# A hybrid layer on one core: the first stage's loads, transposes, modulations and products in another order

## The chip, the cores and the metric

The kernel runs on one core of a Trainium2 chip. The core has a matrix engine (TensorE; PE in the rows, with its weight loads as PEld), a vector engine (VectorE, DVE), a scalar engine (ScalarE, ACT), a general engine (GpSimd, POOL) and SyncE (SP), which here only issues transfers. Each engine works through its own list of instructions in order; semaphores join them. All loads and stores of this stage go through SyncE's queue to the core's 16 DMA engines. The metric is the device time of one execution in microseconds (us), the median of several runs.

## The reference

One layer of a two-branch backbone. 256 context tokens and 1024 latent tokens of width 1024 are RMS-normed and modulated, and one projection gives the columns of an mLSTM head group and of a windowed attention head group. Behind it come both mixers, the output projection, a gated feed-forward mixer and a final norm. The part that the change touches:

```python
sh_a, sc_a, g_a, sh_f, sc_f, g_f = jnp.split((silu(c) @ w_ada + b_ada), 6)      # latent
csh_a, csc_a, ... = jnp.split(silu(c_ctx) @ w_ada + b_ada, 6)                   # context
hc = modulate(rmsnorm(ctx, norm_mix), csh_a, csc_a)     # h * (1 + scale) + shift
hx = modulate(rmsnorm(x, norm_mix), sh_a, sc_a)
u  = h @ w_in      # columns: q/k, v, o, gates of the mLSTM, q, k, v of the attention
```

All in float32. The matrix products are done as three products of halves: every operand is split into a high part (rounded to the engine's faster 32-bit format) and the low rest, and hi*hi + hi*lo + lo*hi are summed (`mm3`).

## The kernel before, in words

The 1280 tokens are ten tiles of 128: tiles 0 and 1 are context, 2 to 9 latent. The first stage, lines 206 to 409, goes as follows. `x_load` brings a tile (0.5 MB) into one of six buffers. `x_norm` squares and sums it on ScalarE, takes the root, and scales the tile on VectorE. `x_trans` turns its eight 128x128 blocks on TensorE into two PSUM banks of the pool `pl` (four banks), and `x_evac` copies the two banks to the transposed store `xT`, one on ScalarE, one on VectorE. `ada_load` brings the modulation weights in pieces (n, q) of 1 MB: n = 0 and 1 are the two halves of the shift, n = 2 and 3 those of the scale, q a half of the contraction. `ada_mm` multiplies a piece with the two conditioning vectors into half of a PSUM pair of the pool `pk`; `ada_vec` turns the row of results into a column per feature (`modS`, `modG`).

`modulate(half, grp, ks)` then makes the projection's operand for one half of the features and one group of tokens (group 0: tiles 0 and 1; group 1: tiles 2 to 5; group 2: tiles 6 to 9): the high part on ScalarE, the full value on VectorE for blocks 1 and 3 of the four and on GpSimd for 0 and 2, and the low part as VectorE's subtraction. Both halves of `modulate` need shift and scale of their features, so half 0 needs n = 0 and 2. `px_mm(c, kts)` multiplies tile c with the small projection weights `w_x` (272 columns: gates, attention keys and values), three matmuls per block of features, 24 per tile; K0 is half 0 and K1 half 1. `px_out(c)` adds the gate bias, copies keys and values out of PSUM into one of three buffers `kv`, rotates the keys on GpSimd, and stores the buffer to memory (`kv_d`). `load_split` loads a weight in two pieces and cuts each into high part (ScalarE) and low part (VectorE).

Among the instructions of the two `manual_schedule` blocks the order is the written one, for each engine of the block: TensorE, VectorE, ScalarE and GpSimd to the end of the stage, SyncE in the inner block only (in the kernel before, to line 385). What is written behind the blocks is placed by the framework's planner, which works with a model of the durations and may put such instructions between those of a block: eight products of the next stage run between those of tiles 7 and 8. The banks: tiles 0, 1 and 6 to 9 use the two banks of the pool `pd`, tiles 2 to 5 those of `pl`. The next stage, `dense`, line 522, starts with a product in `pd` (line 540, tile `pc_`) and then the keys' product in the pair of `pk` (line 548, tile `pp`); its weights come through `load_split` too, in line with the stores on SyncE's queue.

## Time and profile before

| | |
|---|---|
| Time, median of 3 runs | 1319.99 us (1316.4 to 1323.47) |
| The profiled execution | 1321.8 us, span 1319.8 us |
| TensorE busy | 1260.1 us, 95% of the span |
| VectorE, ScalarE, GpSimd busy | 74%, 48%, 20% |
| Mean granted clock of TensorE | 0.985 of full |
| Chain that ended last | TensorE 71%, VectorE 10%, DMA 4%, ScalarE 4%, issue 3% |

The busy share of an engine is an average over stages with different limits; the stage of the change is the first 90 us. The chain is followed back from the last instruction, at each step to what released it. The granted clock is the share of TensorE's clock that it was given: 1.0 is 2.4 GHz, 0.5 is 1.2 GHz.

### The profile page before, as it was taken

The numbers are of one execution on the slowest core, as the hardware profiler recorded it, in microseconds if no ns is written. First come the engines' busy times: TensorE is split into PE (matmuls) and PEld (weight loads), VectorE is DVE, ScalarE is ACT, GpSimd is POOL, SyncE is SP. The second block draws the span as 40 slices with busy tenths as digits, with TensorE's granted clock in tenths as the row PEclk, the third lists the DMA queues.
The fourth block names the chain that finished last, engine by engine and source line by source line (L and its number), as shares of the span: only waits on it lengthen the run. The fifth ranks groups of instructions, "written<-read, shape, count | busy, mean of one in ns | idle before, by whom it ended". The sixth has DMA issues, their size and how long they took to land.

```text
span 1319.8 us, 19433 instructions
## 1 busy us (share of the span) xinstructions
PE 1260.1 (95%) x7047; PEld 1070.9 (81%) x7047; DVE 981.3 (74%) x1752; ACT 636.1 (48%) x1295; POOL 258.8 (20%) x252
## 2 busy tenths in 40 slices
PE   5889999999898999999989999999999999999997
PEld 4689998989898777778768788888888888788886
DVE  4644677767675788997798877777777776877887
ACT  6532546454674566676664333333333333434435
POOL 0450000000035133332420222222122223001000
PEclk8899999999899999999999999999999999999999
DMA  9431435353135412121432323232222326984553
GB/s 362 160 116 33 126 96 176 105 168 101 49 114 164 171 51 96 65 81 48 150 118 67 123 104 112 106 107 99 90 102 106 118 96 218 344 290 158 202 200 134
DMA packets 90225, 175.63 MB, mean 133 GB/s; under 512 B 12746, under 2 KB 29330, under 8 KB 90130
## 3 DMA queue, kind: packets, MB, share of 16 engines
q1 hardware_dynamic: 89842, 173.61, 39.0%
q8 instruction: 55, 0.90, 0.3%
q10 hardware_dynamic: 288, 0.79, 0.2%
q14 instruction: 40, 0.33, 0.1%
HBM read 136.04 MB, written 38.33 MB: 132 GB/s over the span
## 4 chain that ended last, share of the span: by engine, by line
PE 71%; DVE 10%; DMA 4%; ACT 4%; issue 3%; POOL 2%; SPq 0%; ACTq 0%; POOLq 0%; DVEq 0%
PE pd L1857 14%; PE pa L1349 8%; PE pc L1349 8%; PE pp L548 5%; PE pe L1349 4%; PE pd L1349 4%; PE pb L1349 4%; PE u L1119 2%; PE pv L299 2%; PE pv L301 2%; PE pv L300 2%; PE po L299 2%; PE po L301 2%; PE po L300 1%; DVE nm L1067 1%
## 5 line engine op out<-in xcount | busy, mean ns | idle before, releaser
L1451 ACT CAST wh<-Rb 128x1024 fp32r<-128x1024 f32 (+1 forms) x66 | 59.5, 904 | 144.7 <-PE pd L1349 81.6
L1857 PE MATMUL pd<-dh,al 128*128 128x512 f32 x296 | 115.4, 390 | 1.1 <-DVE al L1223 1.1
L1857 PE MATMUL pd<-dl,ah 128*128 128x512 f32 x296 | 115.3, 389 | 0.0
L1857 PE MATMUL pd<-dh,ah 128*128 128x512 f32 x296 | 115.2, 389 | 0.0
L1349 PE MATMUL pc<-hB,wh 128*128 128x512 f32 x344 | 106.0, 389 | 1.1 <-DVE av L1428 1.1
L1349 PE MATMUL pa<-hB,wh 128*128 128x512 f32 x336 | 103.5, 389 | 0.0
L1239 DVE TENSOR_TENSOR wl<-Rb,wh 128x1024 fp32r<-128x1024 f32 (+1 forms) x66 | 68.9, 1045 | 39.4 <-ACT wh L1451 38.8
L1559 POOL TENSOR_TENSOR tt<-vt,tt 128x512 f32<-128x512 f32 x22 | 29.5, 1341 | 321.8 <-ACT tt L1553 321.8
L548 PE MATMUL pp<-hl,wh 128*128 128x512 f32 x256 | 79.3, 405 | 0.0
L1349 PEld LDWEIGHTS pc<-hB,wh 128*128 128x128 f32 x344 | 64.6, 188 | 15.0 <-DVE av L1428 1.6
L299 PE MATMUL pv<-wh,hl 128*128 128x256 f32 x256 | 75.9, 296 | 0.0
L1349 PEld LDWEIGHTS pa<-hB,wh 128*128 128x128 f32 x336 | 63.0, 188 | 13.5 <-ACT sn L1523 0.4
L301 PE MATMUL pv<-wh,hl 128*128 128x256 f32 x256 | 72.4, 283 | 0.0
L300 PE MATMUL pv<-wl,hl 128*128 128x256 f32 x256 | 72.3, 282 | 0.0
L820 POOL TENSOR_TENSOR ta<-z,rope 128x256 f32<-128x256 f32 x16 | 14.3, 895 | 288.7 <-ACT z L816 288.7
L1349 PE MATMUL pc<-hB,wl 128*128 128x512 f32 x172 | 66.9, 389 | 0.0
L1857 PEld LDWEIGHTS pd<-dh,al 128*128 128x128 f32 x296 | 55.6, 188 | 13.4 <-DVE al L1223 1.8
L1349 PE MATMUL pa<-hB,wl 128*128 128x512 f32 x168 | 65.4, 389 | 0.0
L1857 PEld LDWEIGHTS pd<-dl,ah 128*128 128x128 f32 x296 | 55.6, 188 | 11.9 <-DVE dl L1223 0.3
L1857 PEld LDWEIGHTS pd<-dh,ah 128*128 128x128 f32 x296 | 55.6, 188 | 11.4
L299 PE MATMUL px<-wh,hl 128*128 128x256 f32 (+1 forms) x192 | 59.6, 311 | 2.9 <-ACT kr L322 2.9
L301 PE MATMUL px<-wh,hl 128*128 128x256 f32 (+1 forms) x192 | 56.7, 295 | 1.4 <-DVE hl L295 1.4
(1067 smaller groups left out, 3829.2 us busy)
## 6 DMA issues: line engine op xcount, KB each, us to landing
w<-in_w_ada_dram SPq DMA_DIRECT2D x64, 256.0 KB, 2.7
br<-in_w_down_dram SPq DMA_DIRECT2D x25, 512.0 KB, 6.0
Ra<-in_w_up_dram SPq DMA_DIRECT2D x22, 512.0 KB, 3.6
Rb<-in_w_up_dram SPq DMA_DIRECT2D x22, 512.0 KB, 3.6
ar<-act_s SPq DMA_DIRECT2D x44, 256.0 KB, 3.3
act_a<-tt SPq DMA_DIRECT2D x33, 256.0 KB, 2.0
act_s<-tt SPq DMA_DIRECT2D x33, 256.0 KB, 2.0
wr<-in_w_h_dram SPq DMA_DIRECT2D x16, 512.0 KB, 4.5
```

What stands on the lines that cost most here:

```text
L299: T.matmul(ps, st_hi, mv_hi, start=first, stop=False)
L300: T.matmul(ps, st_hi, mv_lo, start=False, stop=False)
L301: T.matmul(ps, st_lo, mv_hi, start=False, stop=last)
L548: T.matmul(pp[:, 512 * n:512 * n + 512], wkq[sw][:, kt, cs], hl[n][part][:, kt, :], start=kt == 0 and sw + part == 0, stop=kt == KT - 1 an ...
L820: G.tensor_tensor(out=ta[:].rearrange("p (h e) -> p h e", h=4), in0=q4, in1=rp_(1), op=ALU.mult)
L1067: V.tensor_reduce(out=self.nm[:, j:j + 1], in_=self.sv[j], axis=AX.X, op=ALU.max, negate=True)
L1119: T.matmul(self.u[:], vv[:, c, self.g], part[i][:, kk * 2 * P:(kk + 1) * 2 * P], start=kb + m == 0, stop=kb == last and m == 1)
L1239: sub = lambda e, o, x, y: e.tensor_tensor(out=o, in0=x, in1=y, op=ALU.subtract)
L1349: T.matmul(ps[:], wt[sw][:, j, ks], hB[part][:, blk, kt, :], start=first and kt == 0 and sw + part == 0, stop=last and kt == 3 and sw == 1 ...
L1451: S.copy(wt[0][:], src)
L1559: G.tensor_tensor(out=self.tt[:, h2_], in0=self.vt[:], in1=self.tt[:, h2_], op=ALU.mult)
L1857: T.matmul(ps[:], ac[sa][:, js], w[sw], start=first and n == 0, stop=last and n == 2, skip_group_check=not fresh)
```

## The change

The loads stand in another order: tiles 0 to 5, then both pieces of n = 0, half the weights `w_x`, both pieces of n = 2, the other half, then tiles 6 to 9, n = 1 and n = 3. Norm, transposes and copies of tiles 6 to 9 stand behind the first products of tiles 0 to 3. The weights' two halves are cut at two places. `spin(n)` issues n transposes of the identity matrix into a bank of `pl` that nothing reads; 12, 5 and 7 of them stand ahead of and between the products and rows of n = 2. The order of the four blocks in a product is 1, 3, 0, 2. Tiles 6 and 7 accumulate in the pair of `pk` that held the rows of n = 1 and 3, tiles 8 and 9 in `pl`. The inner block, with SyncE's written order, now reaches to the last product of tile 7 and so takes in the stores of tiles 0 to 5; behind it the products of tiles 8 and 9 are written with the outputs between them.

```diff
@@ -138,7 +138,7 @@
 
     st = p1.enter_context(tc.tile_pool(name="st", bufs=2))
 
-    def load_split(src, w, rawf=None, split=True, alloc=True):
+    def load_split(src, w, rawf=None, split=True, alloc=True, now=range(2)):
         room = lambda: [st.tile([P, KT, XW], F32R, name=n, tag=n)[:].rearrange("p a b -> p (a b)")[:, :KT * w]
                         .rearrange("p (k f) -> p k f", k=KT) for n in ("wh", "wl")]
         hi, lo = room() if alloc else (None, None)
@@ -158,7 +158,7 @@
                 load(q)
                 cut(q)
             return hi, lo
-        for q in range(2):
+        for q in now:
             load(q)
 
         def rest(qs=range(2)):
@@ -168,6 +168,7 @@
             for q in qs:
                 cut(q)
             return hi, lo
+        rest.load = load
         return rest
 
 
@@ -217,16 +218,17 @@
         V.reciprocal(rstd[:, c:c + 1], rstd[:, c:c + 1])
         V.tensor_scalar(out=xi[:], in0=xi[:], scalar1=rstd[:, c:c + 1], scalar2=None, op0=ALU.mult)
 
-    def x_trans(c):
-        xi = xis.pop(c)
-        for q in range(2):
+    def x_trans(c, qs=range(2)):
+        xi = xis[c]
+        for q in qs:
             pts[c, q] = pl.tile([P, 4, P], F32, name="pt", tag="l")
             for k in range(4):
                 kt = 4 * q + k
                 T.transpose(pts[c, q][:, k, :], xi[:, kt * P:(kt + 1) * P], ident[:])
 
-    def x_evac(c):
-        for q, e in enumerate((S.copy, V.tensor_copy)):
+    def x_evac(c, qs=range(2)):
+        for q in qs:
+            e = (S.copy, V.tensor_copy)[q]
             e(xT[:, 4 * q:4 * q + 4, c * P:(c + 1) * P], pts.pop((c, q))[:])
 
     def bc(ap, n):
@@ -303,12 +305,16 @@
     pxs = {}
 
     def px_mm(c, kts):
-        if kts[0] == 0:
-            pool, tag = (pl, "l") if 2 <= c < 6 else (pd, "d")
-            pxs[c] = pool.tile([P, 512], F32, name="px", tag=tag)
+        if c not in pxs:
+            if c in (6, 7):
+
+                pxs[c] = pas[-1][:, 512 * (c - 6):512 * (c - 6) + 512]
+            else:
+                pool, tag = (pl, "l") if c >= 2 else (pd, "d")
+                pxs[c] = pool.tile([P, 512], F32, name="px", tag=tag)
         px = pxs[c]
         for kt in kts:
-            mm3(px[:, :XW], hsl(0, kt, c), hsl(1, kt, c), wX[0][:, kt, :], wX[1][:, kt, :], kt == 0, kt == KT - 1)
+            mm3(px[:, :XW], hsl(0, kt, c), hsl(1, kt, c), wX[0][:, kt, :], wX[1][:, kt, :], kt == K0[0], kt == K1[-1])
 
     def px_out(c):
         px = pxs.pop(c)
@@ -331,82 +337,111 @@
             G.tensor_tensor(out=kvv[:, :, 1], in0=tv[:, 1, :, 0], in1=tv[:, 0, :, 1], op=ALU.add)
         nc.sync.dma_start(kv_d[c], kv[:])
 
-    K0, K1 = range(4), range(4, 8)
+    K0, K1 = (1, 3, 0, 2), (5, 7, 4, 6)
+
+
+    def spin(n):
+        if "spin" not in pxs:
+            pxs["spin"] = pl.tile([P, 512], F32, name="spin", tag="l")
+        for _ in range(n):
+            T.transpose(pxs["spin"][:, 0:P], ident[:], ident[:])
+
     with tc.manual_schedule(engines={mybir.EngineType.PE, mybir.EngineType.DVE, mybir.EngineType.Activation,
                                      mybir.EngineType.Pool}):
         with tc.manual_schedule(engines={mybir.EngineType.SP}):
-            for c in range(3):
+            for c in range(6):
                 x_load(c)
-            ada_load(0, 0)
-            for c in range(3, 6):
-                x_load(c)
-            ada_load(0, 1)
+            ada_load(0, 0); ada_load(0, 1)
+            wX = load_split(I["w_x"], XW, split=False, alloc=False, now=(0,))
+            ada_load(2, 0); ada_load(2, 1)
+            wX.load(1)
             x_norm(0)
             x_norm(1); x_trans(0); x_evac(0)
             x_load(6)
             x_norm(2); x_trans(1); x_evac(1)
-            ada_mm(0, 0)
             x_load(7)
             x_norm(3); x_trans(2); x_evac(2)
-            x_load(8); ada_load(2, 0)
+            x_load(8)
             x_norm(4); x_trans(3); x_evac(3)
-            x_load(9); ada_load(2, 1)
-            wX = load_split(I["w_x"], XW, split=False, alloc=False)
+            x_load(9)
+            ada_mm(0, 0)
             x_norm(5); x_trans(4); x_evac(4)
             ada_mm(0, 1)
-            x_norm(6); x_trans(5); x_evac(5); ada_vec(0)
-            ada_load(1, 0); ada_load(1, 1); ada_load(3, 0); ada_load(3, 1)
+            x_trans(5); x_evac(5)
+            ada_load(1, 0); ada_load(1, 1)
+            wXf, wX = wX, wX((0,))
+            ada_vec(0)
+            spin(12)
+            ada_mm(2, 0)
+            ada_mm(2, 1)
+            spin(5)
+            ada_load(3, 0); ada_load(3, 1)
             nc.sync.dma_start(rw[:], I["rw"][0:1, 0:536].broadcast_to([P, 536]))
-            x_norm(7); x_trans(6); x_evac(6)
-            x_norm(8); x_trans(7); x_evac(7)
-            ada_mm(2, 0)
-            x_norm(9); x_trans(8); x_evac(8)
-            ada_mm(2, 1)
-            x_trans(9); x_evac(9); ada_vec(2)
+            nc.sync.dma_start(rope[:], I["rope"])
+            ada_vec(2)
+            spin(7)
             modulate(0, 0)
-            wX = wX()
+            px_mm(0, K0)
+            px_mm(1, K0)
+            modulate(0, 1)
+            x_norm(6)
+            px_mm(2, K0)
+            px_mm(3, K0)
+            x_norm(7)
+            x_trans(6); x_evac(6)
             ada_mm(1, 0)
-            px_mm(0, K0)
-            modulate(0, 1)
+            x_norm(8)
+            x_trans(7); x_evac(7)
+            x_norm(9)
             ada_mm(1, 1)
-            px_mm(1, K0)
+            x_trans(8); x_evac(8)
             ada_vec(1)
-            px_mm(2, K0)
             ada_mm(3, 0)
-            hl.append(hl_(1))
-            modulate(0, 2, (0, 1))
-            px_mm(3, K0)
-            ada_mm(3, 1)
-            px_mm(4, K0)
-            ada_vec(3)
-            px_mm(5, K0)
-            nc.sync.dma_start(rope[:], I["rope"])
+            x_trans(9); x_evac(9)
+            wXf((1,))
             wkq = load_split(I["w_h"][0, 0], 256, split=False)
             nc.sync.dma_start(tri[:], I["cst"][:, 1:3])
-        modulate(1, 0)
-        px_mm(0, K1)
-        px_mm(1, K1)
-        modulate(1, 1)
-        px_out(0)
-        px_mm(2, K1)
-        modulate(0, 2, (2, 3))
-        modulate(1, 2, (0, 1))
-        px_out(1)
-        px_mm(3, K1); px_out(2)
-        modulate(1, 2, (2, 3))
-        px_mm(4, K1); px_out(3)
-        wkq = wkq()
-        px_mm(5, K1); px_out(4)
-        px_out(5)
-        amf = xin.tile([P, D], F32, name="amf", tag="xi")[:, :2 * P].rearrange("p (a b) -> p a b", a=2)
-        nc.sync.dma_start(amf, I["cst"][:, 5:7])
+            hl.append(hl_(1))
+            px_mm(4, K0)
+            modulate(0, 2, (1, 3))
+            ada_mm(3, 1)
+            px_mm(5, K0)
+            ada_vec(3)
+            modulate(0, 2, (0, 2))
+            modulate(1, 0)
+            px_mm(6, K0)
+            px_mm(7, K0)
+            px_mm(0, K1)
+            px_mm(1, K1)
+            modulate(1, 1)
+            px_out(0)
+            px_mm(2, K1)
+            px_out(1)
+            px_mm(3, K1)
+            modulate(1, 2, (1, 3))
+            px_out(2)
+            px_mm(4, K1)
+            modulate(1, 2, (0, 2))
+            px_out(3)
+            px_mm(5, K1)
+            wkq = wkq()
+            px_out(4)
+            px_mm(6, K1)
+            px_out(5)
+            px_mm(7, K1)
+            amf = xin.tile([P, D], F32, name="amf", tag="xi")[:, :2 * P].rearrange("p (a b) -> p a b", a=2)
+            nc.sync.dma_start(amf, I["cst"][:, 5:7])
+        px_out(6)
+        px_mm(8, K0 + K1)
+        px_out(7)
         V.tensor_scalar(out=rwc("gain"), in0=rwc("gain"), scalar1=0.5, scalar2=None, op0=ALU.mult)
         V.tensor_copy(identr[:], ident[:])
+        px_mm(9, K0 + K1)
+        px_out(8)
         V.tensor_copy(identb[:], ident[:])
         V.tensor_copy(amask[:], amf)
         V.tensor_scalar(out=nsink[:], in0=rwc("sink"), scalar1=-1.0, scalar2=None, op0=ALU.mult)
-        for c in range(6, NCH):
-            px_mm(c, range(8)); px_out(c)
+        px_out(9)
     p0.close()
 
 
```

## Rows read from the trace of the kernel before

**Rows 1.** Windows. Columns: stretch, length, busy time of each engine (count), clock, DMA share, GB/s.
```profile
core 0: us, PE busy (x) PEld busy (x) DVE busy (x) ACT busy (x) POOL busy (x), PEclk, DMA share, GB/s
9.30:24.85 15.55, 12.16 (x80) 8.88 (x80) 9.83 (x21) 12.63 (x29) 0.00 (x0) 0.99 1.03 400
24.85:31.65 6.80, 6.21 (x28) 3.54 (x32) 4.04 (x8) 3.85 (x8) 0.00 (x0) 0.52 1.04 397
31.65:38.50 6.85, 3.89 (x33) 2.15 (x25) 4.71 (x11) 5.05 (x8) 3.75 (x4) 0.98 1.04 385
38.50:45.30 6.80, 6.25 (x27) 4.34 (x28) 5.43 (x8) 4.41 (x8) 3.31 (x2) 0.52 1.06 379
45.30:74.40 29.10, 27.01 (x207) 24.16 (x206) 17.05 (x34) 13.76 (x24) 12.40 (x15) 1.00 0.09 30
74.40:82.60 8.20, 5.28 (x34) 4.38 (x32) 2.04 (x11) 1.68 (x9) 5.09 (x13) 1.00 0.70 204
82.60:87.20 4.60, 4.59 (x24) 4.59 (x25) 1.53 (x2) 0.30 (x2) 3.50 (x8) 0.63 0.34 121
87.20:170.00 82.80, 82.80 (x568) 76.48 (x567) 46.21 (x134) 32.65 (x81) 3.11 (x4) 1.00 0.31 89
```

**Rows 2.** Timeline of the head: start, length, engine, line, operation; in brackets idle time before.
```profile
21.30 0.95 PE L270 MATMUL pa<-sel,ym 128*128 128x2 f32 x8
...
31.07 1.19 PE L261 MATMUL pa<-wa,ym 128*32 128x512 f32 x8
...
34.59 2.08 ACT L293 ACTIVATE hc<-xT,modS,modG 128x256 fp32r<-128x256 f32 x4 [1.11 <-DVE modG L276]
...
35.24 1.57 DVE L295 TENSOR_TENSOR hc<-ym,hc 128x256 fp32r<-128x256 f32 x3
...
37.71 0.39 PE L299 MATMUL px<-wh,hc 128*128 128x272 f32 x1 [2.23 <-ACT wh L153]
39.05 0.59 PE L300 MATMUL px<-wl,hc 128*128 128x272 f32 x1 [0.94 <-DVE wl L154]
```

**Rows 3.** Timeline of TensorE: steps of the operations; the last row from the chain.
```profile
20.37 1.09 PE L226 MATMUL pt<-ident,xi 128*128 128x128 f32 x8
...
40.12 0.43 PE L301 MATMUL px<-wh,hc 128*128 128x272 f32 x1
...
41.48 0.43 PE L301 MATMUL px<-wh,hc 128*128 128x272 f32 x1
...
48.40 1.06 PE L261 MATMUL pa<-wt,ym 128*32 128x512 f32 x8
...
62.07 0.29 PE L300 MATMUL px<-wl,hl 128*128 128x272 f32 x1
...
69.63 0.29 PE L300 MATMUL px<-wl,hl 128*128 128x272 f32 x1
...
90.27 9.09 PE pp L548 x40
```

**Rows 4.** Chain that ended last, the store behind tile 6's product: start, length, what.
```profile
77.20 4.83 DMA kv_d<-kv
```

**Rows 5.** Timeline of ScalarE and VectorE: squares of two tiles, scaling of one.
```profile
20.99 1.06 ACT L215 ACTIVATE ym<-xi 128x1024 bf16<-128x1024 f32 x1
...
22.84 1.06 ACT L215 ACTIVATE ym<-xi 128x1024 bf16<-128x1024 f32 x1
...
22.69 0.75 DVE L218 TENSOR_SCALAR xi<-xi,rstd 128x1024 f32<-128x1024 f32 x1
```

**Rows 6.** Issue of ada 2's first piece; its size and time from issue to landing.
```profile
16.09 0.43 SPq L250 DMA_DIRECT2D wa<-in_w_ada_dram  x1
...
wa<-in_w_ada_dram SPq DMA_DIRECT2D x1, 1024.0 KB, 8.0
```

**Rows 7.** Windows of transposes alone (line 226) and modulation products alone (line 261).
```profile
28.25:31.65 3.40, 1.97 (x8) 1.57 (x8) 0.54 1.02 394
...
28.25:31.65 3.40, 1.57 (x12) 0.20 (x8) 0.54 1.02 394
```

**Rows 8.** Waits of SyncE's queue: in total, times, longest.
```profile
SPq L149 <- DVE wl L154: 27.2, 3, 20.6
```

## The prediction

> **What bounds the kernel now.** I read the page first: TensorE is busy for 95% of a span of 1319.8 us, and it holds 71% of the chain that ended last. Any gain must therefore be time in which TensorE stands still or runs slowly. The edits lie in the first 90 us, so the second view is the table of windows over that stretch [rows 1]. From 87.20 on TensorE is busy without a gap (82.80 of 82.80 us at full clock): whatever moves 87.20 moves everything behind it by as much. Before 87.20 it is otherwise. The first product of the input projection starts at 37.71 [rows 2]; until then TensorE has done only transposes and the small modulation products.
>
> From 37.71 to the last projection product's end at some 87.2 are 49.5 us. Their work at full clock: 61 matmul starts lie between 62.07 and 69.63 [rows 3], so a projection matmul is 0.126 us, and 240 of them (10 token tiles x 24) are 30.3; three modulation halves (a row of eight matmuls is 1.06, some 1.0 start to start [rows 3]) 3.0; two of the small row products at some 0.8 each (0.95 with its tail [rows 2]) 1.6; and eight key products of the next stage, done early in a gap, 1.8 at 0.227 each (40 in 9.09 [rows 3]). Sum 36.7, so 12.8 us are lost. Where: from 38.50 to 45.30 the granted clock is 0.52, its lower level, 1.2 GHz [rows 1]; there a matmul takes 0.227 (six steps from 40.12 to 41.48 [rows 3]), which costs some 2.8 from 39.05 on. From 82.60 it is at 0.63 for 4.60 us, another 1.5. Idle time is 2.1 from 45.30 to 74.40 and 2.9 from 74.40 to 82.60 [rows 1], and 0.9 is the wait for the weights' low part, to 39.05 [rows 2]. The remaining 2.6 or so are short hand-overs between groups. The 2.9 are a chain, read in order of time: the two PSUM banks that the last four tiles share are freed by copies which wait for a buffer that a store has to empty, and that store took 4.83 us, to 82.03 [rows 4].
>
> Because the eight early key products are not lost work, the old start of the next stage counts as 87.2 - 1.8 = 85.4.
>
> **The head, in the new order.** The first six tiles run as before through the end of tile 5's transposes at 21.30 and the small row product behind it, to 22.25 [rows 2, 3]; only the place of a modulation product between tiles changes, and TensorE idles there anyway (12.16 busy of 15.55 [rows 1]). ScalarE has less to do: a token tile takes it 1.85 us (20.99 to 22.84 [rows 5]), and tiles 6 to 9 (7.4 us) move behind the first products. The cast and subtraction of half the projection weights, 1.1 + 1.5, take their place; both are over by some 25, before their user.
>
> Then comes the scale row (ada 2). Its data now has ahead of it six tiles of 0.524 MB, two pieces of 1.05, half the weights (0.557) and its own two pieces, with 0.16 of constants 8.06 MB. In the kernel before, the first piece of ada 2 had 8.03 MB up to its end and landed at 16.09 + 8.0 = 24.1 [rows 6]. So the second piece lands at some 24.2. Twelve idle transposes stand ahead: 8 transposes start to start are 0.93 (20.37 to 21.30 [rows 2, 3]), so 12 are 1.4, to 23.7; the first half ends at 24.7, and the second can start, its data just there. The transposes thus cost nothing at full clock; at half they take 2.8 and all starts some 2 us later. Later data would hide that too, so the bounds are 0 and +2; I take 0.
>
> From the start of the same second product to the modulation's start were 31.07 to 34.59, 3.5 us, and 0.65 more to the first subtraction [rows 2]. The second and third lots of idle transposes (5 and 7, 0.6 and 0.8 us) stand in that wait. So the first product starts at 24.7 + 3.5 + 0.65 = 28.9 instead of 37.7, its weights ready.
>
> **From there to the next stage.** TensorE has left: 240 projection matmuls 30.3; the transposes of tiles 6 to 9, now behind the first product, 3.8; four modulation halves 4.0; two small row products 1.6: 39.7. Hand-overs as before 2.6, and waits for subtractions in the first tile and at the two places where a new group starts, 1.5 (before, such waits made most of the 2.1). That is 28.9 + 39.7 + 4.1 = 72.7.
>
> What else could be last? VectorE's busy time from 31.65 to 87.20 was 30.8; with four tiles' scaling and copying (1.6 each: 0.75 [rows 5], a copy of about as much, and a reciprocal), 37 at most: 28.5 + 37 = 65. ScalarE's 25.2 [rows 1] + 7.4 end at 61. Both have cover of 8 us or more; if VectorE lost its cover, each late tile would hold TensorE by the part of its 1.85 us that the matmuls ahead don't fill, four times, 0 to 6 us. GpSimd has the rotary work of tiles 2 to 9 last; nothing of the projection waits for it except through buffers. All loads that the stage needs were in by 45.30 in the old order (the DMA share falls from 1.06 to 0.09 [rows 1]), and the bytes are the same; the last modulation piece, needed at some 46, ends with the same sum of bytes. SyncE's queue has x 6 to 9 behind the transposes of tiles 0 to 3, over by 19, and holds a backlog then, so those waits starve nothing.
>
> The banks: tiles 6 and 7 go to the pair that held the modulation rows, free once those are read; 8 and 9 take those of tiles 2 and 3. So the 2.9 idle and the slow 4.60 behind it go. Late next is the pair's next user, the key products, which now wait for tile 7's copies; they begin 3 us after the last projection product (90.27 against 87.2 [rows 3]), some 9 us after tile 7's last product, two tiles of 3.0 standing between. I take 0, with 0 to 5 as bounds (the store of 4.83 [rows 4] as the nearest row).
>
> The clock: the old order lost it twice, each time behind idle gaps. In the sum above TensorE is nearly always busy from 14 to 73. I allow one stretch as at 82.60 (1.5); the bounds are 0 and 7 (all from 28.9 to 45 at the lower level: 16 us, of which 1 - 0.126/0.227 is lost). End: 74.2. Gain 85.4 - 74.2 = 11.2.
>
> The profiled execution took 1321.8; 11.2 less is 1310.6. It stood 1.8 above the median of 1319.99, so the time forecast is 1309.
>
> The Trainium skill (TensorE: Matmul & The Clock Gate, Part 4, on transposes) says that transposes do not bring the full clock, because they do not count as work in the usual way. From 28.25 to 31.65, at 0.54, transposes filled 1.97 and modulation products 1.57 [rows 7], and behind it the clock is full [rows 1]: with transposes the larger part it rose, so the trace leans against the rule; no row has transposes alone. By the rule the idle transposes would be worthless, which is the second case below.
>
> **The rivals.** (A) as above: 1309, own range 1304 to 1313; chance 0.61. (B) The clock stays down: while products wait in turn for VectorE's subtractions and late transposes for their tiles, TensorE runs at 1.2 GHz to about 45 as it did before to 45.30. For it: both old losses came behind gaps of 1 to 3 us; against: the order puts transposes and modulation products into the gaps. The loss is 7 instead of 1.5: gain 5.7, 1314; if the idle transposes run slowly too, 1316. I write 1315; chance 0.17. (C) The stores take back part: three buffers for ten tiles and GpSimd's lag hold tile 7's copies until 77 to 80, TensorE idles up to 3 and then runs 1.5 slower: 1313, chance 0.12. (D) Slower: SyncE's queue is served in order, and the weight loads in it have already waited 20.6 us for VectorE [rows 8]. If the planner puts the next weights' loads ahead of the stores of tiles 4 and 5, those loads wait for slots that only the end of the projection frees, the stores wait behind them, and tile 7's copies and the key products behind those. It decides once the copies come after 77 + 11 = 88; with the wait of 20.6 and a slow restart, 1327; chance 0.05. (E) The work moves but the order laid out behind it costs as much: 1320, chance 0.05.
>
> **How the numbers follow.** A measurement of this kernel tells 0.5%, 6.6 us, from no change. Faster by more: A 0.59, B 0.05, C 0.07, together 0.71. Within: A 0.02, B 0.12, C 0.05, E 0.04, together 0.23. Slower: D 0.05, E 0.01, together 0.06. The range 1303 to 1318 holds A, B and C nearly whole and leaves out D and E.
>
> **What would show it.** First product at 28 to 30 (right) or beyond 33 (the head is wrong). Granted clock full from 18 to 73, or 0.5 somewhere between 29 and 45 (B). No wait of a projection matmul for a copy. Last projection product ending at 72 to 76; key products directly behind. From there on the same work in as much time, to 0.5%. I am wrong if the stage ends before 78 and the span isn't shorter by the difference.

## The result, and the profile after

The changed kernel takes 1311.01 us (median of 9 runs, 1308.92 to 1315.33), the kernel before in the same session 1319.48 (9 runs). The ratio is 0.9941, with a 95% interval of 0.9924 to 0.9958: faster by 5.5 to 10.0 us. Forecast were 1309, range 1303 to 1318. The profiled execution's span is 1306.9 us, before 1319.8.

The timeline of TensorE in the changed kernel, in the columns of [rows 2]: the head, the place where the late waits are, and the end of the stage. Line 263 is the modulation products, 272 the small row product, 347 the idle transposes, 301 to 303 the helper of the three-part products (the projection's when they write `px` or `pa`). Line 575 is the first product of the next stage, which by the source makes the context's keys; some expectations below call it the value columns. Line 583 makes the latent tokens' keys.

```profile
20.30 0.95 PE L272 MATMUL pa<-sel,ym 128*128 128x2 f32 x8
21.11 1.51 PE L347 MATMUL spin<-ident 128*128 128x128 f32 x12
23.10 2.08 PE L263 MATMUL pa<-wa,ym 128*32 128x512 f32 x16 [0.48 <-DVE modS L275]
25.11 0.77 PE L347 MATMUL spin<-ident 128*128 128x128 f32 x5
25.93 1.05 PE L272 MATMUL pa<-sel,ym 128*128 128x2 f32 x8
26.85 0.96 PE L347 MATMUL spin<-ident 128*128 128x128 f32 x7
28.15 0.39 PE L301 MATMUL px<-wh,hc 128*128 128x272 f32 x1 [0.34 <-ACT hc L295]
...
64.99 0.39 PE L303 MATMUL pa<-wh,hl 128*128 128x272 f32 x1 [0.66 <-DVE hl L297]
66.28 0.39 PE L303 MATMUL pa<-wh,hl 128*128 128x272 f32 x1 [0.64 <-DVE hl L297]
...
74.05 0.28 PE L575 MATMUL pc__1022<-hc,wh 128*128 128x256 f32 x1
...
78.39 0.73 PE L583 MATMUL pp<-hl,wh 128*128 128x512 f32 x2 [1.30 <-ACT kr L328]
...
89.40 0.28 PE L301 MATMUL pc__1101<-hc,wh 128*128 128x256 f32 x1
```

The first projection product starts at 28.15 (37.71 before [rows 2]) and the last projection product has handed over at 74.05. The last line, the context's value columns, is the mark that I use from here on: it is the first product behind the keys' products, and the same work lies ahead of it in every version, but for the idle transposes. Before, it stood here:

```profile
99.20 0.28 PE L299 MATMUL pc__1078<-hc,wh 128*128 128x256 f32 x1
```

So the stage ends 9.8 us earlier. The windows of the changed kernel, in the columns of [rows 1], show that TensorE has few gaps and never loses its clock: 1.00, that is 2.4 GHz, in every stretch. Of the three stretches at or near 1.2 GHz in [rows 1] (0.52, 0.52, 0.63) none is left.

```profile
24.85:31.65 6.80, 6.25 (x46) 5.14 (x43) 4.40 (x10) 4.74 (x9) 3.85 (x4) 1.00 1.03 401
29.00:38.50 9.50, 9.40 (x67) 7.47 (x68) 7.55 (x14) 7.91 (x16) 2.52 (x3) 1.00 1.04 388
38.50:45.30 6.80, 6.17 (x49) 3.76 (x47) 3.85 (x8) 4.07 (x9) 0.41 (x1) 1.00 0.88 322
45.30:60.00 14.70, 14.37 (x110) 12.92 (x109) 13.18 (x27) 10.37 (x18) 5.18 (x6) 1.00 0.16 53
60.00:74.40 14.40, 13.09 (x102) 12.65 (x101) 6.79 (x17) 5.92 (x15) 10.09 (x18) 1.00 0.24 56
74.40:82.60 8.20, 6.90 (x41) 5.97 (x40) 4.11 (x11) 4.67 (x11) 5.54 (x10) 1.00 0.49 165
82.60:87.20 4.60, 4.60 (x22) 3.82 (x21) 2.93 (x9) 0.54 (x2) 2.76 (x8) 1.00 0.39 117
87.20:170.00 82.80, 82.80 (x569) 76.39 (x568) 47.41 (x139) 31.19 (x86) 0.00 (x0) 1.00 0.34 99
```

From the mark to the end the span of before has 1220.6 us, that of after 1217.5; in the other profiles below it lies between 1216.8 and 1224.1, whatever was edited. The stage gives the gain, and the profiled pair's 12.9 us is 9.8 and the scatter of the rest.

### The profile page after: what moved, and what is told of

Same layout as the page of the kernel before. It is cut to its first block, busy times and chain, and to the rows that moved or that the text cites. A ratio compares the mean times of both kernels' runs of the same rounds, so it can differ in the third digit from the quotient of the medians.

```text
span 1306.9 us, 19479 instructions
## 1 busy us (share of the span) xinstructions
PE 1255.5 (96%) x7071; PEld 1068.6 (82%) x7071; DVE 980.7 (75%) x1752; ACT 635.3 (49%) x1295; POOL 253.1 (19%) x252
## 3 DMA queue, kind: packets, MB, share of 16 engines
q1 hardware_dynamic: 89842, 173.61, 39.7%
## 4 chain that ended last, share of the span: by engine, by line
PE 53%; DVE 8%; ACT 3%; DMA 2%; issue 2%; POOL 1%; SPq 0%; ACTq 0%; DVEq 0%; POOLq 0%
PE pd L1892 14%; PE pc L1384 8%; PE pa L1384 8%; PE pe L1384 4%; PE pb L1384 4%; PE pd L1384 4%; PE u L1154 2%; PE po L301 2%; PE po L303 2%; PE po L302 1%; DVE nm L1102 1%; PE pt L1131 1%; DMA ar<-act_s 1%; DVE nm L1103 1%; PE pf L1384 0%
## 5 line engine op out<-in xcount | busy, mean ns | idle before, releaser
L1892 PEld LDWEIGHTS pd<-dh,al 128*128 128x128 f32 x296 | 55.6, 188 | 12.9 <-DVE al L1258 1.5
L1138 ACT CAST ph<-pt 128x512 fp32r<-128x512 f32 (+1 forms) x88 | 45.3, 526 | 21.8 <-PE pt L1131 21.3
L1102 DVE TENSOR_REDUCE nm<-sps 128x1 f32<-128x640 f32 (+1 forms) x64 | 50.0, 783 | 6.3 <-PE sps L1098 5.7
```

Of the source, the lines that this page charges most:

```text
L1102: V.tensor_reduce(out=self.nm[:, j:j + 1], in_=self.sv[j], axis=AX.X, op=ALU.max, negate=True)
L1138: S.copy(self.ph[i][:, :w], self.pt[i][:, :w])
L1892: T.matmul(ps[:], ac[sa][:, js], w[sw], start=first and n == 0, stop=last and n == 2, skip_group_check=not fresh)
```

## The experiments

Each ratio is to the kernel before, run beside it. That took 1318.2 to 1320.9 us from session to session, so rows are compared by their ratios and marks, not by their medians. The first product and the mark are from that run's profile, in us.

| run | first product | mark | median | ratio, 95% interval |
|---|---|---|---|---|
| kernel before | 37.71 | 99.20 | 1319.48 | 1 |
| changed kernel | 28.15 | 89.40 | 1311.01 | 0.9941 (0.9924 to 0.9958) |
| changed kernel, again | 28.45 | 89.77 | 1313.57 | 0.9937 (0.9916 to 0.9957) |
| without idle transposes | 28.45 | 89.52 | 1312.65 | 0.9937 (0.9915 to 0.9958) |
| blocks in order | 29.36 | 89.88 | 1311.92 | 0.9940 (0.9927 to 0.9954) |
| scale row late | 34.74 | 95.52 | 1316.30 | 0.9963 (0.9947 to 0.9980) |
| old banks | 28.69 | 95.11 | 1317.06 | 0.9976 (0.9960 to 0.9992) |
| before, banks alone | 38.17 | 99.37 | 1317.75 | 0.9980 (0.9963 to 0.9997) |
| the same, 8 and 9 in `pd` | 38.28 | 103.29 | 1321.39 | 1.0032 (1.0014 to 1.0051) |
| before, banks and end order | 37.52 | 93.99 | 1313.65 | 0.9961 (0.9942 to 0.9979) |
| keys in own room | 28.54 | 88.24 | 1309.83 | 0.9922 (0.9909 to 0.9936) |
| and mask early | 28.26 | 87.94 | 1310.91 | 0.9928 (0.9913 to 0.9944) |
| shift before cut | 28.20 | 87.89 | 1310.28 | 0.9936 (0.9916 to 0.9956) |
| and 12 idle transposes fewer | 28.15 | 87.85 | 1309.79 | 0.9932 (0.9912 to 0.9953) |

**The changed kernel again**, as the measure for the next ones.

> The changed kernel again, as the base for its neighbours. Both theories: 1311 us, ratio to the kernel before 0.993 to 0.9955; last projection product ends at 73.9 to 74.6, key products done (first product of the context values) at 89 to 90, clock full from about 13 to 170.

It repeats in every point: the keys' product waits 1.34 us for tile 7's copy, the mark is at 89.77, the clock is full through the stage.

**Without the idle transposes.**

```diff
-            spin(12)
...
-            spin(5)
...
-            spin(7)
```

> The 24 idle transposes are left out. TensorE then has some 2.0 us of idle time ahead of the scale row's first product (21.1 to 23.1), 0.8 between its second product and its row, 1.4 ahead of the first projection product. Theory 1 (they hold the clock): the granted clock falls to 0.5 for 3.4 to 6.8 us somewhere between 24 and 35, the projection ends 2 to 3 us later (76 to 77), time 1313 to 1314. Theory 2 (they do nothing for the clock, as the Trainium skill's page on TensorE has it, or there is work enough without them): clock as in the changed kernel, projection's end at 73.5 to 74.3, time 1310 to 1311.5.

Both theories were half right. One window over the same 7.85 us, from the first product to tile 6's first transpose (at 36.30 in both), first the changed kernel, run again, then the version without:

```profile
28.45:36.30 7.85, 7.58 (x48) 6.45 (x49) 7.57 (x15) 6.94 (x13) 3.37 (x4) 1.00 1.04 389
```

```profile
28.45:36.30 7.85, 7.85 (x48) 7.67 (x49) 7.58 (x15) 6.95 (x13) 3.38 (x4) 0.78 1.04 388
```

The clock did fall, to 1.2 GHz for 3.4 us. But the 48 matmuls end at the same time, because the third busy time, VectorE's, is 7.57 and 7.58 of 7.85 us: its subtractions pace this stretch. The matmul that needs the last of them starts at 34.56 in the changed kernel and at 34.60 in this one. At full clock the 48 need 6.0 us (0.126 each); the changed kernel spends the other 1.8 in short waits, nearly all for VectorE, and the restarts behind them; this one spends them in slow matmuls. The idle transposes hold the clock and are worth nothing here.

**The order of the blocks.**

```diff
-    K0, K1 = (1, 3, 0, 2), (5, 7, 4, 6)
+    K0, K1 = (0, 1, 2, 3), (4, 5, 6, 7)
```

> The changed kernel, but each product takes its blocks of features in the order 0, 1, 2, 3 and not 1, 3, 0, 2; GpSimd makes the full values of blocks 0 and 2, VectorE those of 1 and 3. Theory 1 (the order lets TensorE start on VectorE's blocks while GpSimd is still at its own): the first product's low part waits for GpSimd's block, the first two tiles end 0.7 to 1.5 us later, and since VectorE's subtractions bound the stretch behind it, half of it or less is left at the context value product (0 to 0.8 us later than 89.4 to 89.8); the median is within 1 us of the changed kernel. Theory 2 (the order carries a real part of the gain): the context value product starts 2 us or more later and the median is 2 us or more above the changed kernel.

The first product comes 0.9 us later (29.36, with the row's idle time 1.33 against 0.34), but not for GpSimd: the row names ScalarE, which still makes the high parts in the order 1, 3, 0, 2, and its third, block 0's, ends at 29.3. At tile 6's first transpose half of the delay is left (36.76 against 36.30). The last projection product hands over 0.8 later than in the changed kernel's second run (75.21 against 74.39), and at the mark only 0.1 is left, since the keys' product behind it now waits 0.63 us for tile 7's copy instead of 1.34. Theory 1 held in size: the order is worth under 1 us, and in this kernel nothing that the median shows, because a later wait swallows it.

**The scale row late**: its pieces and the projection weights behind tiles 6 to 9 in the queue.

```diff
-            wX = load_split(I["w_x"], XW, split=False, alloc=False, now=(0,))
-            ada_load(2, 0); ada_load(2, 1)
-            wX.load(1)
...
             x_load(9)
+            wX = load_split(I["w_x"], XW, split=False, alloc=False, now=(0,))
+            ada_load(2, 0); ada_load(2, 1)
+            wX.load(1)
```

> The loads of the scale row (ada 2) and of the projection weights stand behind those of tiles 6 to 9 again, so that 2.1 MB more come ahead of them; all else as in the changed kernel. Theory 1 (the head is bound by the bytes ahead of the scale row): at 0.39 MB per us the first projection product starts 5.4 us later, 33 to 34, the clock may fall behind the gap, the key products end 4 to 6 us later (93.5 to 95.5), time 1315 to 1317. Theory 2 (what binds the stage is VectorE and the engines' work, the loads are hidden): first product later by less than 2 us, time within 1.5 us of the changed kernel.

The rows of TensorE's waits in this run:

```profile
26.82 1.93 PE L263 MATMUL pa<-wa,ym 128*32 128x512 f32 x8 [4.02 <-DMA wa<-in_w_ada_dram]
29.44 1.93 PE L263 MATMUL pa<-wa,ym 128*32 128x512 f32 x8 [0.69 <-DMA wa<-in_w_ada_dram]
34.74 0.39 PE L301 MATMUL px<-wh,hc 128*128 128x272 f32 x1 [0.35 <-ACT hc L295]
```

The first product comes 6.3 us later than in the changed kernel run beside it and the mark 5.75 later, so a start of the projection that is late by that much is paid for nearly whole (the keys' wait takes up the rest, 0.8 us instead of 1.34). What the new order of loads gives is this earlier start.

**The old banks**, with the rest of the change (the early first halves of tiles 6 and 7 need the new ones and go too).

```diff
-            if c in (6, 7):
...
-                pxs[c] = pas[-1][:, 512 * (c - 6):512 * (c - 6) + 512]
-            else:
-                pool, tag = (pl, "l") if c >= 2 else (pd, "d")
-                pxs[c] = pool.tile([P, 512], F32, name="px", tag=tag)
+            pool, tag = (pl, "l") if 2 <= c < 6 else (pd, "d")
+            pxs[c] = pool.tile([P, 512], F32, name="px", tag=tag)
...
-            px_mm(6, K0)
-            px_mm(7, K0)
...
-            px_mm(6, K1)
+            px_mm(6, K0 + K1)
...
-            px_mm(7, K1)
+            px_mm(7, K0 + K1)
```

> Tiles 6 to 9 take the two PSUM banks of tiles 0 and 1 again, so tiles 6 and 7 can only start behind the copies of 0 and 1 and tiles 8 and 9 behind those of 6 and 7; the rest of the new order stays. Theory 1 (the banks are a part of their own): the waits for a copy come back, 2 to 3 us idle in front of tile 8 or 9, perhaps a slow stretch behind it; eight or so key products slip into the gap; the key products end 3 to 5 us later than in the changed kernel (92.5 to 94.5), time 1314 to 1316. Theory 2 (the earlier loads are the whole gain): within 1 us of the changed kernel.

TensorE's waits:

```profile
51.82 0.39 PE L301 MATMUL px<-wh,hc 128*128 128x272 f32 x1 [1.17 <-ACT hc L295]
53.78 0.59 PE L303 MATMUL px<-wh,hc 128*128 128x272 f32 x1 [1.45 <-DVE hc L297]
...
73.50 0.40 PE L301 MATMUL px<-wh,hl 128*128 128x272 f32 x1 [1.95 <-ACT kr L324]
78.89 0.39 PE L301 MATMUL px<-wh,hl 128*128 128x272 f32 x1 [1.62 <-ACT kr L324]
```

The waits for copies (`kr`) are back, and two waits for the operand at 51 to 54 are new: the first halves of tiles 6 and 7 had filled that time. From the second of them on the clock is at its lower level, to 59.2, 6.8 us in all, which neither the kernel before nor the changed one has at this place. The mark is 5.3 us later than in the run beside it, a little more than theory 1 had.

**Banks alone, on the kernel before.** Three runs, since the first two didn't do what I had meant.

```diff
-            pool, tag = (pl, "l") if 2 <= c < 6 else (pd, "d")
-            pxs[c] = pool.tile([P, 512], F32, name="px", tag=tag)
+            if c in (6, 7):
+                pxs[c] = pas[-1][:, 512 * (c - 6):512 * (c - 6) + 512]
+            else:
+                pool, tag = (pl, "l") if c >= 2 else (pd, "d")
+                pxs[c] = pool.tile([P, 512], F32, name="px", tag=tag)
```

> The kernel before with one edit: tiles 6 and 7 accumulate in the pair of pk that held the modulation rows, tiles 8 and 9 in pl, loads and order of the rest as before. Theory 1 (the banks are a part of the gain that stands by itself): no projection product of tiles 6 to 9 waits for a copy of the tile two ahead of it; the 2.9 us of idle time from 74.40 to 82.60 and the slow stretch from 82.60 go, the last projection product ends at 80 to 81.5 (a little less work ahead of it than 87.2, since the eight early key products move behind it), the context value product starts 4 to 5 us earlier than in the kernel before (94 to 95.5), and the median is 1315.5 (1314 to 1317.5), half of the whole gain. Theory 2 (the banks are worth something only once the head is early; here the keys' product then waits for tile 7's copies and takes the time back): the context value product at 97.5 or later, the median within 1.5 us of the kernel before.

The mark is at 99.37: no gain, as in theory 2, but not for its reason (the ratio leaves room for a small gain, which the mark doesn't show). The planner put the next stage's first product, the context's keys, between tiles 6 and 7, before its weights were cut; TensorE waited 0.78 and 0.74 us for the cut, and the clock was at 0.51 and 0.50 from 72.80 to 79.60. I took that for the cause and blocked it, with tiles 8 and 9 in `pd`:

```diff
-                pool, tag = (pl, "l") if c >= 2 else (pd, "d")
+                pool, tag = (pl, "l") if 2 <= c < 6 else (pd, "d")
```

> The kernel before with one edit, the banks again, but placed so that the planner can't put the next stage's value columns between the tiles: tiles 6 and 7 in the pair of pk, tiles 8 and 9 in the two banks of pd, which they hold until they are copied. Theory 1 (the banks are worth some 5 us by themselves; the run with tiles 8 and 9 in pl lost them only because the value columns came into a free bank of pd before their weights were cut, 1.5 us of waits and 6.8 us at the half clock behind them): the products of tiles 6 to 9 follow one another, the last ends at 80 to 81.5, the context value product starts at 93.5 to 95.5 instead of 99.2 to 99.4, median 1313.5 to 1316. Theory 2 (the old head leaves gaps that take the gain whatever the order: the copies of tile 7 wait for the store of 4.83 us and hold the keys' product): the last projection product ends before 82 but the context value product starts at 97 or later, median within 1.5 us of the kernel before.

Slower than before, which neither theory had. TensorE at tile 7's first product:

```profile
71.91 0.28 PE L301 MATMUL pa<-wh,hl 128*128 128x272 f32 x1
77.97 0.59 PE L299 MATMUL pa<-wh,hl 128*128 128x272 f32 x1 [5.77 <-ACT kr L325]
```

Tile 7's products wait for tile 6's copies, though the two use different banks: the pair is one tile to the framework, and in this kernel the copies of 6 are written ahead of the products of 7. Those copies end at 77.91. They stand on ScalarE behind the weights' cut and the copies of tiles 4 and 5, and the last wait ahead of them, 1.10 us, is for a store. Behind the gap the clock is at 0.50 from 78 to 82. The context's keys in the run ahead had only filled this hole. The change writes both tiles' products ahead of both tiles' copies, so the third run has that order too:

```diff
-        for c in range(6, NCH):
-            px_mm(c, range(8)); px_out(c)
+        px_mm(6, range(8)); px_mm(7, range(8)); px_out(6)
+        px_mm(8, range(8)); px_out(7)
+        px_mm(9, range(8)); px_out(8); px_out(9)
```

> The kernel before with the banks of the change (tiles 6 and 7 in the pair of pk, 8 and 9 in pl), and at the end the order that the change has too: the products of tiles 6 and 7, then the copies of tile 6, the products of 8, the copies of 7, and so on. In the two runs before it the copies of tile 6 stood ahead of the products of tile 7, which share the pair as one tile with it and so waited 5.77 us for them. Theory 1 (banks and order of the end together are worth 4 to 5 us on the old head): the products of tiles 6 to 9 follow one another, the last ends at 80.5 to 81.5 instead of 87.2, the context value product starts at 94 to 96 (with up to 2 us of wait of the keys' product for tile 7's copies), median 1313.5 to 1316.5. Theory 2 (the store of tile 7's buffer takes it all back on the old head): the last projection product ends by 82, but the keys' product waits 3 us or more behind the value columns, and the context value product starts at 97 or later, median within 1.5 us of the kernel before.

TensorE at the end of this stage, and three of its windows:

```profile
80.08 0.29 PE L301 MATMUL px<-wh,hl 128*128 128x272 f32 x1
80.21 0.28 PE L544 MATMUL pc__997<-hc,wh 128*128 128x256 f32 x1
83.08 0.63 PE L552 MATMUL pp<-hl,wh 128*128 128x512 f32 x2
93.99 0.28 PE L299 MATMUL pc__1076<-hc,wh 128*128 128x256 f32 x1
```

```profile
38.50:45.30 6.80, 6.44 (x29) 4.53 (x30) 5.24 (x8) 4.40 (x7) 3.13 (x2) 0.54 1.06 379
...
74.40:82.60 8.20, 8.20 (x68) 8.20 (x67) 1.88 (x11) 1.84 (x10) 4.90 (x14) 1.00 0.74 213
82.60:87.20 4.60, 4.60 (x25) 3.87 (x24) 3.39 (x9) 3.72 (x7) 4.36 (x8) 1.00 0.31 111
```

The 2.9 us idle and the slow 4.60 of [rows 1] are gone (8.20 busy of 8.20; clock 1.00), the head's slow stretches are still there (0.54), and the mark is at 93.99: 5.2 us for banks and end order alone. The old banks on the new head left 4.1 (99.20 to 95.11). Together 9.3, of 9.4 to 9.8 measured for both, and the ratios agree: 0.9961 times 0.9976 is 0.9937. That the parts simply add is not shown, though. The end order is in both runs, and the one with the old banks has a slow stretch of its own. Taken away one at a time, the early loads cost 5.75 and the banks 5.3, together more than the whole.

**The keys in room of their own**: tiles 5 to 7 are copied into token buffers, free by then.

```diff
-        kv = xp.tile([P, 2 * P], F32, name="kv", tag="kv", bufs=3)
+        kv = (xin.tile([P, D], F32, name="kvx", tag="xi")[:, :2 * P] if c in (5, 6, 7)
+              else xp.tile([P, 2 * P], F32, name="kv", tag="kv", bufs=3))
```

> The changed kernel, but the keys and values of tiles 5, 6 and 7 are copied into token buffers that are free by then, instead of into the three buffers that the stores have to empty. Theory 1 (what held the first keys' product by 1.3 us was tile 7's copy, which stood behind tile 6's copy waiting for a store): the copies of tiles 6 and 7 follow their products, the keys' product starts right behind the value columns' product (77.0 to 77.5 instead of 78.4), the context value product starts at 88 to 88.5, and the median is 1.3 us below the changed kernel (ratio to the kernel before 0.9925 to 0.993). Theory 2 (the store is only one of several things due at that time; GpSimd's lag or the next weights' cut takes its place): the keys' product still waits 0.7 us or more, for another engine, and the median is within 0.6 us of the changed kernel.

ScalarE in the changed kernel, ahead of the keys' product that started at 78.39:

```profile
72.35 0.27 ACT L326 COPY kv<-pa 128x128 f32<-128x128 f32 x1 [1.12 <-DMA kv_d<-kv]
72.51 0.27 ACT L328 COPY kr<-pa 128x128 f32<-128x128 f32 x1
77.91 0.27 ACT L326 COPY kv<-pa 128x128 f32<-128x128 f32 x1 [5.12 <-DMA kv_d<-kv]
78.07 0.27 ACT L328 COPY kr<-pa 128x128 f32<-128x128 f32 x1
```

The wait of 5.12 is tile 7's own copy waiting for the store that empties its buffer, and not only tile 6's ahead of it (1.12). With the edit tile 7's copies are over at 74.30, and TensorE goes from the context's keys into the latent tokens' keys without a wait:

```profile
74.03 0.27 ACT L329 COPY kr<-pa 128x128 f32<-128x128 f32 x1 [0.94 <-POOL ta L332]
```

```profile
77.33 0.63 PE L584 MATMUL pp<-hl,wh 128*128 128x512 f32 x2
```

The mark is 1.2 us earlier than in the changed kernel and 1.5 than in its second run. Theory 1 held in the trace: the store was the wait. The medians stand 1.2 and 3.7 below the two of the changed kernel, which were taken in other sessions, and the ratios' intervals overlap; that this version is faster than the change is shown in the trace and not by the times. Against the kernel before it is the best of all here.

**And the mask early** (VectorE's copy `amask` waits 5.32 us for its data in the run before this, 4.42 in the changed kernel):

```diff
             nc.sync.dma_start(tri[:], I["cst"][:, 1:3])
+            amf = xin.tile([P, D], F32, name="amf", tag="xi")[:, :2 * P].rearrange("p (a b) -> p a b", a=2)
+            nc.sync.dma_start(amf, I["cst"][:, 5:7])
```

> As the run before, and the mask that VectorE copies at the end of the stage is loaded with the other constants ahead of the late products, so that VectorE doesn't stand 4.4 us waiting for it. Theory 1 (VectorE's wait at 78 lies beside TensorE's key products and is off the path): VectorE's gap goes, the context value product starts where it does in the run before (within 0.4 us), and so does the median (within 1 us). Theory 2 (VectorE's late work is what the mLSTM's gates wait for, and they hold TensorE later): the stage ends alike but the median is 2 us or more lower.

VectorE's gap goes (the copy starts at 73.71 instead of 79.40). The mark is 0.3 earlier, as far as the head is (28.26 against 28.54), and the time is the same: off the path.

**The shift's column before the cut, then without the twelve idle transposes.** Both on the version with the keys in own room; the second leaves out `spin(12)` too.

```diff
-            wXf, wX = wX, wX((0,))
             ada_vec(0)
+            wXf, wX = wX, wX((0,))
             spin(12)
```

> The version with the keys of tiles 5 to 7 in room of their own, and one swap: the shift's column (modS) stands ahead of the cut of the first half of the projection weights on VectorE, not behind it. Theory 1 (the scale row's product waited for modS, which had the cut's 1.3 us ahead of it; its data was there): the product starts right behind the twelve idle transposes, 0.5 us earlier (22.6 to 23.1, by the start of the load), and the first projection product 0.5 us earlier; at the end of the stage less than that is left. Theory 2 (its data came last, as I had predicted): it waits for a DMA instead, starts within 0.2 us of where it did, and nothing else moves.

> As the run before, and the twelve idle transposes ahead of the scale row's product are left out (the five and the seven behind it stay), so that only data or modS can hold it. Theory 1 (data was there well ahead): the product starts at 21.7 to 22.3, 1.3 to 1.8 us earlier than with the cut ahead, in one run of 16; the first projection product at 26.6 to 27.2. At the stage's end 0.5 us or more of it is left, the median 0.5 to 1.5 us below the version with the keys in room of their own, if VectorE's subtractions leave it. Theory 2 (the data lands at 23 to 24): the product waits for a DMA to 23 or later, between its first and its second half if not ahead of it, and the median is that of the version with the keys in room of their own within 1 us.

The scale row's products, in the first and in the second of the two runs:

```profile
22.64 1.06 PE L263 MATMUL pa<-wa,ym 128*32 128x512 f32 x8
24.21 1.06 PE L263 MATMUL pa<-wa,ym 128*32 128x512 f32 x8 [0.51 <-DMA wa<-in_w_ada_dram]
```

```profile
21.55 1.07 PE L263 MATMUL pa<-wa,ym 128*32 128x512 f32 x8 [0.46 <-DMA wa<-in_w_ada_dram]
24.16 1.06 PE L263 MATMUL pa<-wa,ym 128*32 128x512 f32 x8 [1.54 <-DMA wa<-in_w_ada_dram]
```

In the changed kernel the row was one run of 16 from 23.10, and its wait was put down to VectorE's `modS`. With `modS` out of the way the first half starts earlier, and the second waits for its data until 24.2 all the same; the first product stays at 28.15 to 28.20. The other profiles with this order of the loads and the blocks have it at 28.15 to 28.69, so the 0.3 us to the version that these two build on (28.54) tells nothing. Theory 2 held for the end: the data binds. In the changed kernel `modS` ended its wait just so late that the second half, at 24.1, found its piece landed.

## Why the prediction was right, step by step

**The head.** Forecast: the scale's second piece lands at 24.2, the first product starts at 28.9. The last two runs show that half waiting for its data until 24.16 and 24.21, so the sum of bytes in the queue was right to 0.1 us. The product came at 28.15, 0.75 earlier, mostly because I had let the first half start at 23.7, behind the idle transposes; it started at 23.10. I had the first six tiles' transposes end at 21.30, as before, and they end at 20.30; the wait for `modS`, which I didn't have, took back half of that. The idle transposes cost nothing at full clock (12 in 1.51), as assumed: with and without the twelve the first product starts at 28.20 and 28.15.

**VectorE's cover** failed as a step. I compared VectorE's work with TensorE's up to 65 and found 8 us to spare. In the first 7.85 us behind the first product there is none: VectorE is busy for 7.57 (in the changed kernel's second run) and TensorE's 48 matmuls lose 1.8 us beside it. I had 1.5 for all waits for subtractions. Cover is to be read stretch by stretch, which is the rule that I had set for TensorE and not kept for VectorE.

**GpSimd** failed as a step too: I wrote that nothing of the projection waits for it except through buffers. At tiles 6 and 7 TensorE waits 0.66 and 0.64 us for subtractions, and these are late because VectorE itself waits for GpSimd's full values:

```profile
64.24 0.70 DVE L297 TENSOR_TENSOR hl<-ym,hl 128x512 fp32r<-128x512 f32 x1 [2.90 <-POOL ym L292]
65.53 0.69 DVE L297 TENSOR_TENSOR hl<-ym,hl 128x512 fp32r<-128x512 f32 x1 [0.59 <-POOL ym L292]
```

```profile
61.89 0.88 POOL L331 TENSOR_TENSOR ta<-kr,rope 128x128 f32<-128x128 f32 x2 [6.22 <-ACT kr L328]
...
63.44 2.06 POOL L292 TENSOR_SCALAR ym<-xT,modG,modS 128x512 f32<-128x512 f32 x2
```

GpSimd makes these values (line 292) behind the rotation of tile 2's keys (line 331), as written, and stands idle for 6.22 us ahead of that rotation. No run has the two the other way round, so whether the 1.3 us can be had is not shown.

**The clock.** I allowed 1.5 us for one slow stretch; there was none. (The old order lost the clock not twice, as I wrote, but in three stretches of [rows 1].) From first product to last 45.9 us went by, 39.7 of work and 6.2 lost, where I had 5.6: 1.8 beside VectorE, 1.3 through GpSimd, some 3.1 in hand-overs and smaller waits. So the errors cancelled, more waits against no slow stretch and an early head, and that the end came at 74.05, forecast 74.2, is luck to that extent. Rival B is refuted for this order.

The Trainium skill (TensorE: Matmul & The Clock Gate, Part 4) says that transposes do not bring the full clock, as they do not count as work in the usual way. The run without them bears against it: with all 24 the granted clock stays at 1.00, without them it falls to 0.5 at 28.3. With the last 12 alone it held too, through a gap of 1.54 us at 22.6 (the run with 12 fewer). No run shows whether transposes by themselves would bring the clock up from its lower level. The conclusion that I drew from that rule, that they might be worthless, came true for another cause, VectorE's pace.

**The banks.** No projection product waits any more for the copies of an earlier tile's keys and values; one, at 44.85, waits 0.24 us for a copy of transposed blocks. The banks and the end's order are worth 5.2 us by themselves; I had 2.9 and 1.5 in the old loss, 4.4.

**The next user of the pair.** I took 0 with bounds 0 to 5; it was 1.30. That is rival C, at a third of its size: the store held tile 7's copies to 78 (77 to 80 was its forecast), and the run with room of their own gives it back. Put in, it explains the mark: 99.20 less the forecast gain of 11.2 is 88.0, plus 1.3 is 89.3, measured 89.40. D (the queue's order, slower) came in its first half only, and C's wait lies behind it. Two loads of the next weights, of 0.5 MB each, are issued ahead of tile 4's store, whose buffer tile 7's copy needs:

```profile
70.92 1.00 SPq L149 DMA_DIRECT2D wr<-in_w_h_dram  x2
72.61 2.24 SPq L338 DMA_DIRECT2D kv_d<-kv  x2
```

The loads waited for no room here, so the copy came at 77.91 and not behind 88. But the store issued at 72.61 landed after 5.2 us, the one issued at 70.50, ahead of the loads, after 1.8. That the loads made it slow is likely and not tested. E did not come either, by the length of the rest.

**Time.** A stage gain of 9.8 instead of 11.2 would have made the forecast 1310.4; measured 1311.0. What is left is within the interval.

## What to carry to other kernels

Price a reordering as parts that can be undone one by one: here all but the banks gave 4.1 us and the banks with the order of the end 5.2, of 9.8, and nearly nothing came from the idle transposes and the block order, which look just as purposeful in the code. A part that shows no gain may be hidden behind a later wait, as the block order was. Check an engine's cover in the window behind each new start and not over the stage, because the first products of a stage run at the pace of whoever makes their operands. A wait's named releaser may itself have waited for another engine, so look at its row too; and it may hide a second one that ends at nearly the same time, so move the first away before you count on its time. When one part is tried alone, take the order of instructions along that it needs, since two tiles in one buffer may wait for each other's copies.

## What the runs showed of the hardware

A half-speed stretch can be free: 3.4 us at 1.2 GHz changed neither the end of the stretch (36.30 in both) nor the time. Twelve transposes of an identity in 32 bits take 1.51 us at full clock, 0.12 each, and small as they are the 24 kept 2.4 GHz up through the waits of the head (12 of them did too), where the same order without any lost it.
